# Spreading row scalars with TensorE, and a reordered sparse attention stage, in a two-model transformer stack

## The chip, the cores and the metric

The kernel runs on one core of a Trainium2 chip. The metric is the device time of one execution, in microseconds (us). The weights come from device memory in every execution, about 226 MB of reads.

## The reference

Two small stacks follow one another on a sequence of 512 tokens with 1024 features. The first has a pooling and state space mixer ("even"), a gated convolution mixer ("odd") and a norm ("fn"). The second has two layers, each with a gated feed-forward block ("ffa"), a mixer ("mix"), and a second feed-forward block ("ffb"). The mixer of layer 0 is differential attention beside a recurrent mixer; that of layer 1 is the sparse attention beside an mLSTM. What the change touches is this:

```python
def rmsnorm(x, w, eps=NORM_EPS):
    xf = x.astype(jnp.float32)
    y = xf * lax.rsqrt(jnp.mean(xf * xf, axis=-1, keepdims=True) + eps)
    return (y * w.astype(jnp.float32)).astype(x.dtype)
...
def compress_blocks(z, pe, w1, w2):
    n_cmp = (T - CMP_BLOCK) // CMP_STRIDE + 1
    idx = CMP_STRIDE * np.arange(n_cmp)[:, None] + np.arange(CMP_BLOCK)[None, :]
    blocks = (z[:, :, idx] + pe).reshape(B, G, n_cmp, CMP_BLOCK * d)
    return jax.nn.gelu(blocks @ w1) @ w2
...
    # native_sparse_attention, per block of queries: three softmax branches
    pc = jnp.where(mc, jax.nn.softmax(jnp.where(mc, sc, NEG_INF), axis=-1), 0.0)
    o_cmp = jnp.einsum('bghqn,bgne->bghqe', pc.astype(dt), v_cmp)
    ...
    return gi[..., 0:1] * o_cmp + gi[..., 1:2] * o_slc + gi[..., 2:3] * o_win
```

## The kernel before

Activations lie transposed: features on 128 partitions, the 512 tokens along the free axis, so `x` is eight tiles of 128x512. Every dense product is in split half precision: a weight chunk of 128x1024 is loaded on SP's queue into `st` (L271), ScalarE makes the high half `wh` (L281), VectorE the low half `wl` (L282), and TensorE adds three products per 128-row block, wh·xh, wh·xl, wl·xh (`form1`, L298 to L300, 24 matmuls for one output tile; `form2`, L316 to L318, the same with tokens on the partitions). Three `st` and three pairs `wh`, `wl` are in flight. Each output tile takes one of the eight accumulator banks (`b0` to `b7` in the program, `b` in the rows); the feed-forward blocks use seven of them (`mm=7`), so TensorE can work seven output tiles ahead of the engine that reads them.

Norms are applied late. `norm` scales `x` by its gain into `hh`, `hl`, and the dense products start on that at once. Meanwhile ScalarE squares, VectorE adds (`nsum`, L358), TensorE sums over partitions with a column of ones (L362), and GpSimd takes the power -0.5 (L335). This gives one scalar per token, four columns on 128 partitions (`r`, `rhoc`). To multiply an output tile it has to be a row of 512, repeated on all partitions. `spread` does that: either `rows` (L330) transposes each column, broadcast to 128, on TensorE into a bank and ScalarE copies it out (L378), or, with `far`, SP writes the 2 KB to DRAM (L374) and reads them back broadcast to 128 partitions (L375). The result is `rho`, by which VectorE multiplies each output (L324), and `rb`, which the next norm uses. Before the change all four feed-forward blocks use `far` for both; the two mixers of the second stack use it for `rb` alone. The first feed-forward block also takes in the norm "fn", so it needs two rounds of moments (L362 twice), and scales `x` itself by a spread `rb` in between (L430).

In the last mixer the steps are listed by hand (`START1`, `MIX1`): `s` makes keys with a rotary turn (`rope`: four DMAs `swap` of 64 KB on SP, two products on GpSimd, L988 and L989, a sum on VectorE, L990), `n` values, `f` gates, `c` one compressed branch (0 for keys, 1 for values), `q` a pair of query heads in all three branches, `v`, `k`, `g`, `h` belong to the mLSTM. A compressed branch takes the dense output `sm`, moves it with four DMAs into `zst`, GpSimd adds the position term (`zb`, four adds, L1483), and TensorE multiplies by four chunks of 512 KB, `w` (32-bit matmuls, L1492, 62 columns).

For each pair of heads `nsa_pair` goes through 12 units (four blocks of queries, three branches): scores (L1562), mask and row maximum in one instruction (L996), maximum times -0.125 (L997), exponential (L998), transposes (L1577), a split into halves on ScalarE and VectorE (L1580, L1581), values (L1586). After the third branch of a block of queries six VectorE instructions weigh and add the branches (L1594, L1596).

The order in which each engine issues is set when the program is built: a scheduler places the instructions by a simulated timeline, and some carry a high priority. Each engine then works strictly in its own order, and a waiting instruction holds up all behind it, on SP's queue of DMAs too.

Of the kernel before, what the change touches and what calls it, by code (L numbers as in the profile page):

```python
# [10 lines left out]
F32 = mybir.dt.float32  # L11
F16 = mybir.dt.float16
AF = mybir.ActivationFunctionType
ALU = mybir.AluOpType
# [3 lines left out]
P = 128  # L18
T = 512
# [13 lines left out]
START1 = [('s', 0), ('n', 1), ('c', 0), ('s', 1), ('f', 0), ('c', 1)]  # L33
# [5 lines left out]
PS = 4096.0  # L39
MIX1 = [('q', 0), ('v', 0), ('k', 0), ('g', 0), ('g', 1), ('k', 2), ('h', 0), ('k', 3), ('h', 1), ('g', 3), ('q', 1), ('k', 1), ('q', 2), ('g', 2), ('q', 3), ('v', 1), ('h', 2), ('h', 3)]  # L40
# [144 lines left out]
class Net:  # L185
    def __init__(self, ctx, tc, A, out, taps=None):
        self.tc, self.nc, self.A, self.out = tc, tc.nc, A, out
        self.taps = taps or {}
        nc = self.nc
# [6 lines left out]
        self.rb = self.inv = self.fn = None  # L196
# [136 lines left out]
    def pow(self, x, e, n=4):  # L333
        r = self.small([P, n], "nr2")
        self.nc.gpsimd.tensor_tensor(r, x, (self.half if e < 0 else self.plus)[:, :n], op=ALU.pow)  # L335
        return r
# [44 lines left out]
    def norm(self, i, exact=False, far=False):  # L381
# [4 lines left out]
        g = self.norms[:, i]  # L386
        if exact:
            self.reciprocal()
# [20 lines left out]
        r = self.pow(v, -0.5)  # L409
# [5 lines left out]
        if self.fn is not None:  # L415
# [4 lines left out]
            v = self.small([P, 4], "nv2")  # L420
# [3 lines left out]
            R = self.spread(r, "rb", True)  # L424
            r = self.pow(v, -0.5)
            V.tensor_mul(t, t, r)
        self.rhoc, self.rho = t, self.spread(t, "rho", far)
# [4 lines left out]
        self.reciprocal(v, r)  # L432
        return hh, hl

    def reciprocal(self, v=None, r=None):
        now = v is None
        if now:
            v = self.moments()
            r = self.pow(v, -0.5)
        self.rb = self.spread(r, "rb", not now and self.inv is not None)  # L440
# [38 lines left out]
    def ffn(self, tag, ni, last=0):  # L479
        nc = self.nc  # L480
        with ExitStack() as c:
# [3 lines left out]
            hh, hl = self.norm(ni, far=True)  # L485
# [506 lines left out]
    def soft(self, tk, ps, mask, n, mx, ls, tag, bufs):  # L992
# [476 lines left out]
    def compress(self, s, K, sp, cw, zt):  # L1469
        nc, A = self.nc, self.A  # L1470
        V, G = nc.vector, nc.gpsimd
# [67 lines left out]
    def nsa_pair(self, i, K, nk, yh, yl, q):  # L1539
# [27 lines left out]
        def values(qt, j):  # L1567
# [5 lines left out]
            for hb, pe in enumerate(st.pop((qt, j))):  # L1573
                ps = self.aux()
                at = nk.tile([P, 2, 4, P], F16, name="nat", bufs=3)
                for kt, (k0, kn) in enumerate(ks):
                    nc.tensor.transpose(ps[0:kn, kt * P:(kt + 1) * P], pe[:, k0:k0 + kn], self.ident)  # L1577
                kn, nb = ks[0][1], len(ks)
                v = ps[0:kn, :nb * P].rearrange("p (a b) -> p a b", b=P)
                nc.scalar.activation(at[0:kn, 0, :nb], v, AF.Copy, scale=PS)  # L1580
                V.scalar_tensor_tensor(at[0:kn, 1, :nb], v, PS, at[0:kn, 0, :nb], op0=ALU.mult, op1=ALU.subtract)  # L1581
                for kt in range(nb):
# [228 lines left out]
```

## Time and profile before

| | |
|---|---|
| median of the runs | 2630.56 us (2622.67, 2630.56, 2630.58) |
| profiled execution | 2621.48 us |
| its span, first to last instruction | 2619.7 us |
| mean granted TensorE clock | 0.967 |
| HBM read | 225.57 MB, 89 GB/s over the span |

The profile is of one execution. The busy time of TensorE counts a matmul from its issue to its modelled end, and matmuls overlap; so the distance between starts, and gaps in which nothing runs, tell more than the duration of one. A row of a view in windows gives, for each engine, the busy us and the number of instructions in that stretch, then the granted clock (1.00 is 2.4 GHz, 0.50 is 1.2 GHz).

### The profile page before, as it was taken

Reading aid. Unit: us, or ns where it says so; the run is one execution under the profiler, and the core shown is the slowest. Engines: PE = TensorE matmul, PEld = TensorE weight load, DVE = VectorE, ACT = ScalarE, POOL = GpSimd, SP = SyncE. Lnnn points to the kernel's source line nnn. Section 1 sums busy time; section 2 is a strip of 40 time slices with the busy share of each in tenths; the row PEclk is TensorE's granted clock in tenths of the full one; section 3 lists DMA queues with packets and bytes.
Section 4 is the critical chain, followed back from the end, with each engine's and each line's share of the span. In section 5 each row is a group of like instructions: output and inputs, shape, how many; then the busy total and the mean of one; then the engine's idle time right before and its main releaser. Section 6 shows DMA issues by size and latency. Waiting matters only on the chain.

```text
span 2619.7 us, 36948 instructions
## 1 busy us (share of the span) xinstructions
PE 2489.5 (95%) x14409; PEld 1267.5 (48%) x14409; DVE 1413.3 (54%) x2623; ACT 937.8 (36%) x1619; POOL 722.5 (28%) x625
## 2 busy tenths in 40 slices
PE   6998989989999999999999999999979999999998
PEld 3554434434444556664444444444455555444445
DVE  8945897643333777766333334333335777643334
ACT  3123665423322333334323223332223565433222
POOL 4811861133310333322333103332012110143300
PEclk9889999989999999999999999999989999899999
DMA  4223221233333421123333333333343101333334
GB/s 161 80 55 114 85 68 41 93 96 98 104 110 119 109 70 51 37 63 120 113 99 102 100 103 108 101 105 97 103 119 103 61 24 37 73 117 104 101 99 126
DMA packets 116247, 240.59 MB, mean 92 GB/s; under 512 B 44904, under 2 KB 54248, under 8 KB 116072
## 3 DMA queue, kind: packets, MB, share of 16 engines
q1 hardware_dynamic: 100416, 229.84, 29.1%
q10 hardware_dynamic: 15656, 8.39, 1.2%
q8 instruction: 113, 1.85, 0.3%
q14 instruction: 62, 0.51, 0.1%
HBM read 225.57 MB, written 7.36 MB: 89 GB/s over the span
## 4 chain that ended last, share of the span: by engine, by line
PE 70%; issue 9%; DVE 8%; DMA 5%; POOL 5%; ACT 2%; SPq 1%; POOLq 0%; ACTq 0%; DVEq 0%
PE b L298 14%; PE b L299 14%; PE b L300 14%; PE b L504 4%; PE b L506 4%; PE b L505 4%; POOL cv L921 2%; DVE wl L282 1%; PE b L1149 1%; PE b L1562 1%; PE mm L300 1%; PE mm L299 1%; PE mm L298 1%; PE b L1492 1%; PE b L1065 1%
## 5 line engine op out<-in xcount | busy, mean ns | idle before, releaser
L298 PE MATMUL b<-hh,wh 128*128 128x512 f16 x2096 | 799.6, 383 | 34.7 <-ACT hh L289 7.8
L300 PE MATMUL b<-hh,wl 128*128 128x512 f16 x2096 | 799.6, 382 | 4.1 <-DVE wl L282 4.1
L299 PE MATMUL b<-hl,wh 128*128 128x512 f16 x2096 | 801.8, 383 | 0.4 <-POOL hl L290 0.4
L281 ACT ACTIVATE wh<-st 128x1024 f16<-128x1024 f32 (+6 forms) x432 | 421.9, 978 | 1047.6 <-PE b L299 651.2
L282 DVE SCALAR_TENSOR_TENSOR wl<-st,wh 128x1024 f16<-128x1024 f32 (+6 forms) x432 | 507.5, 1176 | 324.0 <-ACT wh L281 323.2
L299 PEld LDWEIGHTS <-wh 128*128 128x128 f16 x2320 | 229.6, 99 | 303.8 <-issue 47.2
L298 PEld LDWEIGHTS <-wh 128*128 128x128 f16 x2320 | 230.3, 99 | 297.4 <-issue 28.8
L300 PEld LDWEIGHTS <-wl 128*128 128x128 f16 x2320 | 229.9, 99 | 291.6 <-issue 21.6
L504 PE MATMUL b<-fh,wh 128*128 128x512 f16 x660 | 250.1, 379 | 0.0
L505 PE MATMUL b<-fl,wh 128*128 128x512 f16 x660 | 250.1, 379 | 0.0
L506 PE MATMUL b<-fh,wl 128*128 128x512 f16 x660 | 250.1, 379 | 0.0
L493 POOL TENSOR_TENSOR sg<-sg,rho 128x512 f32<-128x512 f32 x88 | 150.8, 1716 | 311.9 <-ACT sg L492 311.9
L290 POOL TENSOR_TENSOR fl<-f,fh 128x512 f16<-128x512 f32 x88 | 142.6, 1620 | 255.2 <-ACT fh L289 255.2
L324 DVE TENSOR_TENSOR sg<-b,rho 128x512 f32<-128x512 f32 x88 | 60.4, 690 | 256.2 <-PE b L300 215.0
L496 DVE SCALAR_TENSOR_TENSOR f<-b,sg 128x512 f32<-128x512 f32 x88 | 60.8, 690 | 237.9 <-PE b L300 225.9
L290 POOL TENSOR_TENSOR hl<-nh,hh 128x512 f16<-128x512 f32 x45 | 57.8, 1291 | 352.2 <-ACT hh L289 352.2
L506 PEld LDWEIGHTS <-wl 128*128 128x128 f16 x660 | 64.6, 98 | 78.0
L505 PEld LDWEIGHTS <-wh 128*128 128x128 f16 x660 | 64.6, 98 | 77.8
L504 PEld LDWEIGHTS <-wh 128*128 128x128 f16 x660 | 64.6, 98 | 77.8
L298 PE MATMUL mm<-hh,wh 128*128 128x512 f16 x224 | 88.1, 397 | 9.3 <-ACT hh L289 7.4
L921 POOL TENSOR_TENSOR cv<-cv,cvt 128x512 f32<-128x512 f32 x60 | 88.3, 1474 | 15.1 <-ACT cvt L920 10.7
L299 PE MATMUL mm<-hl,wh 128*128 128x512 f16 x224 | 88.2, 395 | 3.1 <-DVE hl L290 1.9
(607 smaller groups left out, 3065.9 us busy)
## 6 DMA issues: line engine op xcount, KB each, us to landing
st<-in_gu_a SPq DMA_DIRECT2D x88, 512.0 KB, 3.5
st<-in_gu_b SPq DMA_DIRECT2D x88, 512.0 KB, 3.5
st<-in_dn_b SPq DMA_DIRECT2D x36, 512.0 KB, 3.4
st<-in_dn_a SPq DMA_DIRECT2D x32, 512.0 KB, 3.5
st<-in_od_in SPq DMA_DIRECT2D x24, 512.0 KB, 3.5
st<-in_ab_in SPq DMA_DIRECT2D x22, 512.0 KB, 3.6
st<-in_cd_in SPq DMA_DIRECT2D x16, 512.0 KB, 3.6
st<-in_ev_in SPq DMA_DIRECT2D x15, 512.0 KB, 3.8
```

Source lines behind the costliest of these rows:

```text
L281: nc.scalar.activation(wh[:, s], st[:, s], AF.Copy, scale=WS)
L282: nc.vector.scalar_tensor_tensor(wl[:, s], st[:, s], WS, wh[:, s], op0=ALU.mult, op1=ALU.subtract)
L290: (eng or self.nc.gpsimd).tensor_sub(lo, src, hi)
L298: self.nc.tensor.matmul(ps, wh[:, s], xh[:, k], start=(k == 0), stop=False)
L299: self.nc.tensor.matmul(ps, wh[:, s], xl[:, k], start=False, stop=False)
L300: self.nc.tensor.matmul(ps, wl[:, s], xh[:, k], start=False, stop=(k == kn - 1))
L493: nc.gpsimd.tensor_mul(sg, sg, self.rho)
L496: nc.vector.scalar_tensor_tensor(f, ps, 1.0 / FS, sg, op0=ALU.mult, op1=ALU.mult)
L504: nc.tensor.matmul(ps, wh[:, s], fh[:, k], start=(k == 0), stop=False)
L505: nc.tensor.matmul(ps, wh[:, s], fl[:, k], start=False, stop=False)
L506: nc.tensor.matmul(ps, wl[:, s], fh[:, k], start=False, stop=(k == KF - 1))
L921: G.tensor_add(cv, cv, t)
```

## The change

Four things change.

- `spread` loses its `far` form: every row scalar is spread by four transposes on TensorE and a copy on ScalarE. In the five norms from "ffa" of layer 0 on, the spread of `rb`, which only the next norm needs, is put off until four output tiles later (`later`, `due`, `LATE`).
- A compressed branch is made in two steps, `p` (dense output, DMAs, position term) and `c` (the rest), and other steps stand between them in `START1`. `Q` prepares the first query pair there, and the first `v` moves from `MIX1` to `START1`.
- `soft` folds the factor -0.125 into the masking instruction and takes a minimum, so that L997 goes. It is used in both mixers of the second stack.
- In `nsa_pair` the two heads of a unit share one bank, one copy and one low half where they fit, and the sum over branches is one VectorE product over all three (128x384) and two GpSimd sums. The product's tile shares its buffers with `swap`.

```diff
-START1 = [('s', 0), ('n', 1), ('c', 0), ('s', 1), ('f', 0), ('c', 1)]
+START1 = [('s', 0), ('n', 1), ('p', 0), ('s', 1), ('f', 0), ('Q', 0), ('c', 0), ('p', 1), ('v', 0), ('c', 1)]
+LATE = 4
-MIX1 = [('q', 0), ('v', 0), ('k', 0), ('g', 0), ('g', 1), ...
+MIX1 = [('q', 0), ('k', 0), ('g', 0), ('g', 1), ...
...
+    def later(self):
+        if self.due:
+            self.due[0] -= 1
+            if not self.due[0]:
+                _, v, r = self.due
+                self.due = None
+                self.reciprocal(v, r)
+
     def form1(self, src, kn, xh, xl, w=None):
+        self.later()
...
-    def spread(self, r, name, far=False):
+    def spread(self, r, name):
         t = self.cp.tile([P, T], F32, name=name)
-        if far:
-            d = self.dr.tile([1, T], F32, name=name + "_", bufs=2)
-            self.nc.sync.dma_start(d.rearrange("o (j p) -> (o p) j", j=4), r)
-            self.nc.sync.dma_start(t, d.to_broadcast([P, T]))
-            return t
-        ps = self.rows(r, range(4))
-        self.nc.scalar.activation(t, ps, AF.Copy)
+        self.nc.scalar.activation(t, self.rows(r, range(4)), AF.Copy)
         return t
...
-            R = self.spread(r, "rb", True)
+            R = self.spread(r, "rb")
...
-        self.rhoc, self.rho = t, self.spread(t, "rho", far)
+        self.rhoc, self.rho = t, self.spread(t, "rho")
...
-        self.reciprocal(v, r)
+        if self.inv is None:
+            self.reciprocal(v, r)
+        else:
+            self.due = [LATE, v, r]
...
-        nc.vector.tensor_tensor_reduce(pe[:, :n], ps, mask, 1.0, -3e38, ALU.add, ALU.max, accum_out=mx)
-        nc.vector.tensor_scalar(mx, mx, -0.125, None, op0=ALU.mult)
-        nc.scalar.activation(pe[:, :n], pe[:, :n], AF.Exp, bias=mx, scale=0.125, accum_out=ls)
+        nc.vector.tensor_tensor_reduce(pe[:, :n], ps, mask, -0.125, 3e38, ALU.add, ALU.min, accum_out=mx)
+        nc.scalar.activation(pe[:, :n], pe[:, :n], AF.Exp, bias=mx, scale=-1.0, accum_out=ls)
...
-            for hb, pe in enumerate(st.pop((qt, j))):
+            for hbs in ((0, 1),) if nb < 3 else ((0,), (1,)):
                 ps = self.aux()
                 at = nk.tile([P, 2, 4, P], F16, name="nat", bufs=3)
...
-            for hb in range(2):
-                d = o[:, qt, hb * 64:hb * 64 + 64]
-                V.tensor_scalar(d, po[:, hb, 0], ls[:, hb, 0:1], None, op0=ALU.mult)
-                for j in (1, 2):
-                    V.scalar_tensor_tensor(d, po[:, hb, j], ls[:, hb, j:j + 1], d, op0=ALU.mult, op1=ALU.add)
+            w = nk.tile([P, 2, 3, 64], F32, name="nw", tag="swap")
+            V.tensor_mul(w, po, ls.unsqueeze(3).to_broadcast([P, 2, 3, 64]))
+            d = o[:, qt].rearrange("p (h e) -> p h e", h=2)
+            G.tensor_add(d, w[:, :, 0], w[:, :, 1])
+            G.tensor_add(d, d, w[:, :, 2])
...
-                K["kv"[j] + "cmp"] = self.compress("kv"[j], K, sp, cw, zt)
+                K[j] = self.blocks("kv"[j], cw, zt)
+
+            def compressed(j):
+                K["kv"[j] + "cmp"] = self.compress("kv"[j], K, sp, cw, K[j])
```

The scheduler makes a new order of the whole program from this; up to the first feed-forward block it is the same but for the name of one small tile. In the changed kernel line numbers are higher: L271 is L272, L987 is L994, L1476 is L1482, L1488 is L1499, L1492 is L1503, L330 is L341.

On SP at the start of the first feed-forward block (`in_gu_a`, its first weights; `rb`, `rho` with a number, the copies in DRAM), before:

```order
L271 DMA st<-in_gu_a 128x1024 x8
L374 DMA rb__4326<-nr_4287 128x4x1
L375 DMA rb<-rb__4326 128x512
L271 DMA st<-in_gu_a 128x1024 x3
L374 DMA rb__4345<-nr_4329 128x4x1
L374 DMA rho__4333<-rhoc 128x4x1
L375 DMA rb<-rb__4345 128x512
L375 DMA rho<-rho__4333 128x512
L271 DMA st<-in_gu_a 128x1024 x33
```

and now:

```order
L272 DMA st<-in_od_in 128x1024 x24
L272 DMA st<-in_od_out 128x1024 x8
L272 DMA st<-in_gu_a 128x1024 x44
L272 DMA st<-in_dn_a 128x1024 x2
L272 DMA st<-in_dn_a 128x768
```

Six DMAs are gone, and with them the places where SP stood between weights until a scalar was ready and its copy had landed in DRAM.

On SP in the last mixer, after the weights of the values (`cd_n`) and gates (`cd_g`), before:

```order
L271 DMA st<-in_cd_g 128x320
L271 DMA st<-in_cd_in 128x1024
L374 DMA rb__15544<-nr2n 128x4x1
L375 DMA rb<-rb__15544 128x512
L987 DMA swap<-sm 32x512 x4
L271 DMA st<-in_cd_in 128x1024
L271 DMA st<-in_cd_v 128x1024
L1476 DMA zst<-sm 64x511 x2
L1703 DMA ksx<-ks 64x1024
```

and now:

```order
L272 DMA st<-in_cd_g 128x320
L272 DMA st<-in_cd_in 128x1024
L994 DMA swap<-sm 32x512 x4
L272 DMA st<-in_cd_in 128x1024
L272 DMA st<-in_cd_v 128x1024
L1482 DMA zst<-sm 64x511 x2
L272 DMA st<-in_cd_v 128x1024
L994 DMA swap<-sm 32x512 x2
L1723 DMA ksx<-ks 64x1024
```

The turn of the keys (`swap`) and the move of the compressed branch (`zst`) no longer stand behind the two DMAs of `rb`.

On TensorE at the first matmuls of the compressed keys (`g` are the gates, `w` with a number one 512 KB chunk), before:

```order
L317 MATMUL b_15957<-wl,hh 128x160
L318 LDWEIGHTS hl
L318 MATMUL b_15957<-wh,hl 128x160
L1492 MATMUL b_15754<-zb,w_15755 128x62 x8
L1492 MATMUL b_15754<-zb,w_15765 128x62 x8
L1492 MATMUL b_15754<-zb,w_15775 128x62 x8
L1492 MATMUL b_15754<-zb,w_15785 128x62 x8
L298 LDWEIGHTS wh
```

and now:

```order
L328 MATMUL b_15875<-wl,hh 128x160
L329 LDWEIGHTS hl
L329 MATMUL b_15875<-wh,hl 128x160
L341 MATMUL b_15952<-ident,nrk 128x128 x4
L1503 MATMUL b_16003<-zb,w_16004 128x62 x7
L1448 MATMUL b_15904<-ident,g_15538 4x128
...
L311 MATMUL b_15966<-hh,wl 128x512
L1503 MATMUL b_16003<-zb,w_16004 128x62
L1503 MATMUL b_16003<-zb,w_16014 128x62 x8
L309 LDWEIGHTS wh
```

The 24 dense matmuls of the second keys now stand ahead of this place, where before they came after all four chunks, and dense work stands between the chunks.

## Rows read from the trace of the kernel before

**Rows 1.** the page's first part: busy us, share, instructions.

```profile
PE 2489.5 (95%) x14409; PEld 1267.5 (48%) x14409; DVE 1413.3 (54%) x2623; ACT 937.8 (36%) x1619; POOL 722.5 (28%) x625
```

**Rows 2.** the view in windows, whole core; steady feed-forward is 600:650.

```profile
500.00:552.00 52.00, 40.81 (x175) 18.91 (x174) 25.34 (x38) 16.01 (x21) 7.94 (x7) 0.87 0.28 79
600.00:650.00 50.00, 50.00 (x233) 22.68 (x232) 18.92 (x20) 15.46 (x20) 17.20 (x10) 1.00 0.32 96
850.00:1240.00 390.00, 376.30 (x3516) 230.52 (x3515) 277.27 (x654) 142.94 (x283) 113.42 (x107) 0.98 0.28 75
...
1596.00:1606.00 10.00, 8.27 (x38) 3.46 (x37) 6.10 (x7) 5.85 (x8) 6.63 (x5) 1.00 0.31 108
1929.13:1940.50 11.37, 9.35 (x101) 8.48 (x98) 4.32 (x5) 2.48 (x4) 1.34 (x1) 0.85 0.34 47
1940.50:1953.60 13.10, 0.00 (x1) 0.01 (x1) 3.70 (x3) 2.52 (x3) 7.69 (x7) 0.58 0.43 120
1953.60:1968.40 14.80, 14.16 (x65) 13.85 (x66) 0.32 (x2) 0.00 (x0) 0.62 (x1) 0.50 0.62 195
1968.40:2008.00 39.60, 36.64 (x220) 23.57 (x221) 19.29 (x36) 10.64 (x14) 14.28 (x12) 0.90 0.37 114
2008.00:2250.00 242.00, 227.06 (x1797) 130.18 (x1797) 181.48 (x671) 133.71 (x416) 26.72 (x24) 0.94 0.13 40
2250.00:2310.00 60.00, 54.90 (x249) 24.39 (x248) 37.69 (x49) 27.93 (x39) 21.55 (x15) 0.97 0.47 118
```

**Rows 3.** chain that ended last, pieces in order: start, us, what.

```profile
508.30 7.62 DMA rb__4326<-nr
...
531.47 8.67 DMA rho__4333<-rhoc
540.15 4.78 DMA rho<-rho__4333
...
1927.23 8.38 DMA rb__15544<-nr2n
1935.63 5.09 DMA rb<-rb__15544
1940.79 7.47 DMA zst<-sm
...
1950.78 2.09 POOL ks L290
```

**Rows 4.** timeline of TensorE, 522 to 547: start, us, idle before, releaser.

```profile
527.25 0.99 PE L362 MATMUL b<-ones,nsum 128*128 128x1 f32 x4 [3.84 <-DVE nsum L358]
...
545.70 0.59 PE L298 MATMUL b<-hh,wh 128*128 128x512 f16 x1 [7.35 <-DVE sg L324]
```

**Rows 5.** timeline of VectorE, 505 to 531.

```profile
520.51 2.08 DVE L430 SCALAR_TENSOR_TENSOR x<-x,norms,rb 128x512 f32<-128x512 f32 x3 [7.84 <-DMA rb<-rb__4326]
```

**Rows 6.** line L330 in 1900 to 2000: min, median, max ns.

```profile
L330 PE MATMUL b<-ident,rhoc x4: 272/272/275, 1928.5 to 1928.9; 128*128 128x128 f32 x4
```

**Rows 7.** timeline of SP's queue, 1926 to 1945.

```profile
1936.06 2.42 SPq L987 DMA_DIRECT2D swap<-sm  x4
```

**Rows 8.** timeline of GpSimd, 1930 to 1994.

```profile
1944.00 1.26 POOL L988 TENSOR_TENSOR sm<-sm,c_rope 128x512 f32<-128x512 f32 x1 [10.84 <-DMA swap<-sm]
...
1948.39 2.38 POOL L1483 TENSOR_TENSOR zb<-zst,pe_k 128x248 f32<-128x248 f32 x2 [1.92 <-DMA zst<-sm]
...
1952.83 1.39 POOL L1483 TENSOR_TENSOR zb<-zst,pe_k 128x248 f32<-128x248 f32 x2
```

**Rows 9.** groups by line, TensorE, 2003 to 2009: busy us, mean ns.

```profile
L1492 PE MATMUL b<-zb,w 128*128 128x62 f32 x32 | 3.8, 276 | 1.5 <-POOL nq L290 1.5
```

**Rows 10.** groups by line and shape, VectorE, 2008 to 2250.

```profile
L1596 DVE SCALAR_TENSOR_TENSOR no<-b,nls,no 128x64 f32<-128x64 f32 x64 | 17.4, 272 | 0.5
...
L997 DVE TENSOR_SCALAR nmx<-nmx 128x1 f32<-128x1 f32 x96 | 11.8, 141 | 0.3
...
L1581 DVE SCALAR_TENSOR_TENSOR nat<-b,nat 128x384 f16<-128x384 f32 x16 | 8.7, 549 | 2.0 <-ACT nat L1580 1.9
```

More of the change, by code (lines that the diff above doesn't have):

```diff
@@ L386, in norm @@
         g = self.norms[:, i]
+        assert not self.due
         if exact:
-            self.reciprocal()
+            v = self.moments()
+            self.reciprocal(v, self.pow(v, -0.5))
         if self.fn is not None:
@@ L408, in norm @@
                 v = self.moments()
-        r = self.pow(v, -0.5)
+        keep = lambda: self.cp.tile([P, 4], F32, name="nrk", bufs=3)
+        r = self.pow(v, -0.5, r=keep())
         t = self.cp.tile([P, 4], F32, name="rhoc", bufs=2)
@@ L419, in norm @@
                 w = self.moments(gain, 0.0)
-            v = self.small([P, 4], "nv2")
+            v = self.cp.tile([P, 4], F32, name="nv", bufs=4)
             V.tensor_mul(v, r, r)
@@ L431, in norm, with reciprocal @@
             self.fn = None
-        self.reciprocal(v, r)
+        if self.inv is None:
+            self.reciprocal(v, r)
+        else:
+            self.due = [LATE, v, r]
         return hh, hl
[L435 to L440, printed above, removed]
+    def reciprocal(self, v, r):
+        self.rb = self.spread(r, "rb")
         self.inv = self.cp.tile([P, 4], F32, name="inv", bufs=2)
@@ L1572, in values @@
             ks = [(0, 31)] if j == 0 else [(kt * P, P) for kt in range(qt + 1)]
-            for hb, pe in enumerate(st.pop((qt, j))):
+            kn, nb = ks[0][1], len(ks)
+            pes = st.pop((qt, j))
+            for hbs in ((0, 1),) if nb < 3 else ((0,), (1,)):
                 ps = self.aux()
                 at = nk.tile([P, 2, 4, P], F16, name="nat", bufs=3)
[L1576 to L1582, printed above, removed]
-                    for a, c in ((0, 0), (0, 1), (1, 0)):
-                        v = K["vcmp"][:, c, g * 64:g * 64 + 64] if j == 0 else (
-                            K["nv"][:, c, kt, (j - 1) * P + g * 64:(j - 1) * P + g * 64 + 64])
-                        nc.tensor.matmul(po[:, hb, j], at[0:kn, a, kt], v, start=(kt + a + c == 0),
-                                         stop=(kt == nb - 1 and a == 1))
+                for e, hb in enumerate(hbs):
+                    for kt, (k0, _) in enumerate(ks):
+                        b = e * nb + kt
+                        nc.tensor.transpose(ps[0:kn, b * P:(b + 1) * P], pes[hb][:, k0:k0 + kn], self.ident)
+                na = len(hbs) * nb
+                v = ps[0:kn, :na * P].rearrange("p (a b) -> p a b", b=P)
+                nc.scalar.activation(at[0:kn, 0, :na], v, AF.Copy, scale=PS)
+                V.scalar_tensor_tensor(at[0:kn, 1, :na], v, PS, at[0:kn, 0, :na], op0=ALU.mult, op1=ALU.subtract)
+                for e, hb in enumerate(hbs):
+                    for kt in range(nb):
+                        for a, c in ((0, 0), (0, 1), (1, 0)):
+                            v = K["vcmp"][:, c, g * 64:g * 64 + 64] if j == 0 else (
+                                K["nv"][:, c, kt, (j - 1) * P + g * 64:(j - 1) * P + g * 64 + 64])
+                            nc.tensor.matmul(po[:, hb, j], at[0:kn, a, e * nb + kt], v, start=(kt + a + c == 0),
+                                             stop=(kt == nb - 1 and a == 1))
             if j < 2:
@@ L1773, in mix1 @@
             for step, n in START1 + MIX1:
-                dict(c=packed, s=keys, n=vals, f=gates, Q=query, q=quer, k=qk, v=values, g=gate, h=head)[step](n)
+                dict(p=packed, c=compressed, s=keys, n=vals, f=gates, Q=query, q=quer, k=qk, v=values, g=gate, h=head)[step](n)
             for k in CD_OUT:
```

23 lines of the change are left out of this document (13 added, 10 removed).

## The prediction

> **What bounds the kernel now.** I read the page's engine list first: TensorE is busy 95% of the span, the next engine (VectorE) 54% [rows 1]. Then the windows: in a feed-forward block TensorE runs 233 matmuls in 50 us at full clock, 0.215 us each, with no gap [rows 2], so there nothing but fewer matmuls helps. The change removes no dense matmul. What it can win is time in which TensorE stands, and time at 1.2 GHz after it stood. The windows find these in few places: the start of the first feed-forward block (500 to 552), the start of the sparse attention (1929 to 2008), its inner stretch (2008 to 2250), and little in the starts of the later blocks. The chain of waits names the cause in the first two: the trips of a row scalar through DRAM, and the move of the compressed keys [rows 3]. The timelines give what each engine waited for.
>
> **First feed-forward block.** The trip of `rb` begins at 508.30 and VectorE's scaling of `x` at 520.51, 12.2 us later [rows 3, 5]. In VectorE's order the last two sums of the second round of moments stand behind that scaling, so TensorE, which must sum them over partitions, stands 3.84 us [rows 4]. Then the trip of `rho`, 531.47 to 544.93, is longer than the seven banks last, and TensorE stands 7.35 us more [rows 3, 4]. In all, the 175 matmuls of 500 to 552 would take 37.6 us at the steady rate and took 52: 14.4 us lost, idle and half clock together [rows 2].
> In the new order TensorE does the first moments, 52 dense matmuls (11.2 us), the second moments, 20 more, the transposes of `rb`, 22 more, the transposes of `rho`. So `rho` is asked for about 94 x 0.215 = 20.2 us after the first moments where its arrival came at 544.93 (540.15 + 4.78, rows 3), some 37 us after `rb`'s trip began, and the sums no longer stand behind the scaling. From just ahead of that trip's start (508.30), say 507, this is 527 to 529, before the banks ran out (538.35, less the 3.84 of idle before it: 534.5). Neither idle stays. What is late next is `wl`: the eight scalings now stand between two of them on VectorE, eight times 0.69 us (2.08 for three, rows 5) is 5.5 us against 5.2 us for one output tile, with two pairs ahead; I allow 1 us. Gain 13.4; bounds 8 (if a bank still runs dry) and 14.4.
>
> **Later feed-forward blocks.** There the trip ends within the seven banks; only a `wl` or `wh` queued behind the first use of `rho` is late. 1596 to 1606 has 1.7 us idle, and 2250 to 2310 has 5.1, of which I put 3 on `rho` [rows 2]. Gain 4.7; bounds 0 and 7.
>
> **Price of the spreads.** Eleven spreads leave DRAM: three in the first block, two in each of the three others, one `rb` in each of the two mixers. Four transposes start within 1928.5 to 1928.9 and take 0.272 us each, pipelined [rows 6]: 0.5 us of TensorE for each spread, 5.5 in all, and none of it hidden, since TensorE is the bound. Each also holds all that stands behind it if the power on GpSimd is late; the new order puts 26 dense matmuls (5.6 us) between moments and `rho` in the later blocks, against about 3 us of small work, so I take no wait; up to 1.5 us each, 16 in all, stays in the range.
>
> **Start of the sparse attention.** Loss before, by window [rows 2]: 2.0 idle and about 1 from the clock up to 1940.5; 13.1 idle; then the 64 matmuls of the compressed keys take 14.8 us at 1.2 GHz, where 32 of the same take 3.8 us at full clock [rows 9], so 7.2 lost; then 3.0 idle and 4.0 from a clock of 0.90. Sum 30.3.
> The 13.1 us end with the position term: SP's queue stood 8.38 us for `rb`, then read it back (1935.63), then issued the swaps (1936.06) and, last, `zst` at 1940.79 [rows 3, 7]; GpSimd took the swapped keys at 1944.00 and finished two pairs of adds, with the split of `ks` in between, at 1954.2 [rows 3, 8]. Without `rb` that chain moves up by something between 0 and 8.4 us; I take 5.5, what lies between the swaps' issue and the keys' being ready when the first product with `rho` is out, a little after 1930. So `zb` is ready near 1948. TensorE does the second keys first (24 x 0.215 = 5.2 us, partly in the 2.0 idle) and one spread, and comes to the compressed keys near 1944.2. It stands 4 us instead of 13.1 (bounds 1 and 9.4). A standstill like this costs some 2 us of half clock (500 to 552 lost 0.13 x 52 = 6.8 us of clock with two of them, idle time included). From there the four chunks have dense work between them, so a late chunk or a late gate row hides in part; I leave 4 us for these. Loss after 10, gain 20; bounds 7 (9.4 idle, 7.2 half clock, 7 of waits) and 27.
>
> **Inner stretch of the sparse attention.** 242 us, 15 idle, clock 0.94 [rows 2]. The 96 scalings by -0.125 go: 96 x 0.141 = 13.5 us of VectorE. The 96 instructions of the branch sum (0.272 each, 26 us) become 16 products over 384 columns, near 0.55 us as the split of 384 columns takes [rows 10], 9 us. Thirty-two of 96 copies and low halves merge with a neighbour. VectorE sheds over 30 of 181 us, but TensorE is the bound there too, and its waits on VectorE are a part of the 15 us idle. Against it stand 32 sums on GpSimd, which no row shows at this size: adds of 248 columns took 0.70 to 1.2 us each [rows 8], so 0.35 to 0.6; they run beside other work but for the last ones before the transposes of the output, where they replace VectorE instructions of about the same length. And 40 of the matmuls that filled this stretch now stand before it. I take a gain of 6; bounds -8 and 16.
> GpSimd's adds show a cost of sharing: the same two adds took 2.38 us while VectorE made low halves `wl`, and 1.39 us after [rows 8], 0.5 us more for each add. The Trainium skill (SBUF — State Buffer, "SBUF: two separate sides") says that GpSimd shares a pair of ports with VectorE, and that a VectorE instruction with two SBUF inputs and a GpSimd instruction lock each other out for the whole of an instruction. By that rule the trace's 2.38 us is no accident, since `wl` is made of `st` and `wh`, both in SBUF; the low halves of the softmax read one of their inputs from a bank, and would not lock. This is the third rival below.
>
> **Differential attention** (850 to 1240): the order is new in detail, the mix of work is the same, 13.7 us are idle [rows 2]. I take 0; bounds -6 and 6.
>
> **Sum.** 13.4 + 4.7 + 20 + 6 - 5.5 = 38.6 us from the profiled 2621.5: 2582.9. The median of the timed runs lies 9 us above the profiled one, with one run at 2622.67 beside it; I do not know which the changed kernel's median will meet, and add 2: 2585.
>
> **Rivals.**
> 1. The compressed keys still come late (chance 0.17). For: `zst` now stands behind two weight loads of 512 KB on SP, and GpSimd's order around it is unchanged; 8.38 of standstill is an upper end of what goes. Against: the second keys are ahead in any case. Gain 7 there instead of 20, and spreads that wait 0.5 us each: 2585 + 13 + 6 = 2604.
> 2. More comes back (0.13): the clock stays full through the whole start and the inner stretch gives 16: 2585 - 7 - 10 = 2568.
> 3. The sums on GpSimd and VectorE hold each other up all through the inner stretch (0.05): 32 sums at 0.5 us more each (2.38 against 1.39 for two) is 16 us on the chain that the transposes of the output wait for: 2585 + 16 = 2601. Against: the dense steps in this stretch are few, and so is `wl`. By the skill's rule, named above, the lock would come with `wl` alone, which is why the chance is small.
> 4. Slower than before (0.04): the branch product takes `swap`'s two buffers, so the turn of the next query pair must wait for the sums of the pair before, and nothing covers it. The whole chain from swaps to split took 16.8 us for `ks` (1936.06 to 1950.78 + 2.09, rows 3, 7). Three of them in the open, with the clock at half behind each (7.2 us lost at most, as above), are 3 x 24 = 72 us: 2585 + 72 = 2657. It decides from about 12 us each on. Against: the new order has dense work at those places.
> That the spreads do not pay at all is no rival: the gaps of 3.84 and 7.35 us name them.
>
> **How the numbers follow.** The forecast has 0.61, with its own range 2572 to 2600. The range 2562 to 2611 takes in rivals 2 and 3 and the first, and most of what the unknown order of the mixers can do; the slower case stays outside. Within 0.3% of 2630.6 (about what repeated timings of this kernel differ by) means 2622.7 to 2638.5: 0.05, from rival 1 with a bad order elsewhere. Faster 0.91, slower 0.04.
>
> **What would show it.** Right: no wait of TensorE for `nsum` or `sg` after the first moments at 507; the idle before the first compressed matmul at 1 to 9 us, with dense work between chunks; the granted clock of 1929 to 2008 above 0.85 throughout; the inner stretch 0 to 16 us shorter. Wrong: a wait of TensorE at the transposes of `rhoc` or `nrk` of over 1 us, a gap of over 9 us before the compressed keys, VectorE waiting for GpSimd's `no`, or swaps late on SP with TensorE idle.

## The result and the profile after

The changed kernel takes 2562.23 us (median of 2556.68 to 2567.23) against 2628.84: the ratio is 0.975, with a 95% interval of 0.9722 to 0.9778. Beside other runs on another chip it is 0.977 (0.9746 to 0.9794). Forecast were 2585 with a range of 2562 to 2611: the direction is right, the time lies 0.23 us inside the range's lower edge, and the gain is half as large again as forecast. The profiled execution spans 2558.1 us (2619.7 before).

The page's first part, of the changed kernel, answers to [rows 1]:

```profile
PE 2462.0 (96%) x14453; PEld 1259.9 (49%) x14453; DVE 1397.3 (55%) x2383; ACT 940.7 (37%) x1598; POOL 734.6 (29%) x657
```

To see where the time went, both programs are cut at the first sum over partitions of each norm (L362 before, L373 now). The view in windows, kernel before: first feed-forward block, first mixer, two feed-forward blocks, last mixer, last feed-forward block. The first number after a window is its length, the last three are the granted clock, the DMA share and GB/s.

```profile
506.00:866.50 360.50, 349.31 (x1604) 158.74 (x1604) 138.09 (x164) 105.78 (x132) 85.16 (x60) 0.98 0.35 107
866.50:1237.10 370.60, 356.90 (x3423) 221.25 (x3422) 267.03 (x634) 135.87 (x273) 109.80 (x100) 0.98 0.27 70
1237.10:1580.30 343.20, 342.62 (x1593) 155.68 (x1592) 128.91 (x140) 104.73 (x129) 82.43 (x52) 1.00 0.34 103
1580.30:1924.30 344.00, 342.27 (x1614) 156.28 (x1612) 126.84 (x139) 101.73 (x127) 82.82 (x53) 1.00 0.35 104
1924.30:2277.30 353.00, 317.58 (x2363) 191.81 (x2361) 236.89 (x753) 166.21 (x463) 61.19 (x52) 0.90 0.22 66
2277.30:2598.40 321.10, 317.77 (x1561) 152.50 (x1561) 117.88 (x128) 98.34 (x120) 76.38 (x46) 1.00 0.36 108
```

The same six stages of the changed kernel:

```profile
502.90:848.30 345.40, 345.40 (x1616) 158.41 (x1615) 137.01 (x164) 107.65 (x135) 84.91 (x60) 1.00 0.36 110
848.30:1224.80 376.50, 360.72 (x3425) 226.11 (x3425) 265.62 (x602) 136.00 (x274) 111.00 (x100) 0.98 0.24 69
1224.80:1568.20 343.40, 343.40 (x1601) 156.73 (x1601) 128.96 (x140) 105.84 (x131) 82.70 (x52) 1.00 0.34 102
1568.20:1910.90 342.70, 342.70 (x1621) 157.29 (x1620) 126.72 (x139) 103.11 (x129) 82.58 (x53) 1.00 0.34 103
1910.90:2218.60 307.70, 291.81 (x2368) 178.46 (x2366) 220.69 (x545) 163.74 (x432) 72.55 (x84) 0.98 0.25 75
2218.60:2536.90 318.30, 318.30 (x1569) 153.56 (x1569) 118.47 (x128) 99.16 (x122) 76.43 (x46) 1.00 0.36 108
```

Subtract the lengths: 15.1, -5.9, -0.2, 1.3, 45.3 and 2.8 us, 58.4 together. In all four feed-forward blocks TensorE's busy time now equals the window: it stands nowhere, and the list of its waits in them is empty. The last mixer brings three quarters of the gain. It falls into a start and a rest; the cut is after 520 of its matmuls, the same count in both kernels (not quite the same matmuls, since the new list moves some). Before, then after:

```profile
1924.25:2013.85 89.60, 70.89 (x523) 55.50 (x521) 31.87 (x64) 18.81 (x31) 25.90 (x22) 0.79 0.40 112
2013.85:2277.33 263.48, 246.77 (x1842) 136.37 (x1840) 205.02 (x690) 147.47 (x433) 35.29 (x30) 0.94 0.16 50
```

```profile
1910.94:1976.93 65.99, 62.57 (x523) 47.33 (x521) 34.09 (x58) 19.77 (x31) 21.68 (x22) 0.95 0.53 164
1976.93:2218.64 241.71, 229.23 (x1845) 131.10 (x1846) 186.60 (x487) 143.94 (x402) 50.87 (x62) 0.99 0.17 50
```

The start gains 23.6 us, the rest 21.8. What the first compressed matmuls wait for, answering to the 13.1 us window of [rows 2], stands in TensorE's timeline of the changed kernel, and SP's queue there answers to [rows 7] and the 1940.79 of [rows 3]:

```profile
1931.30 2.00 PE L1503 MATMUL b<-zb,w 128*128 128x62 f32 x14 [2.63 <-POOL zb L1489]
```

```profile
1917.24 3.43 SPq L994 DMA_DIRECT2D swap<-sm  x4
...
1921.88 1.16 SPq L1482 DMA_DIRECT2D zst<-sm  x2
```

Counted from the stage's first sum over partitions, the swaps leave after 6.3 us (11.8 before) and the first compressed matmul runs after 20.4 (29.4 before).

### The profile page after: what moved, and what is told of

It is laid out like the page before. It is cut to its first block, busy times and chain, and to the rows that moved or that the text cites. A ratio compares the mean times of both kernels' runs of the same rounds, so it can differ in the third digit from the quotient of the medians.

```text
span 2558.1 us, 36794 instructions
## 1 busy us (share of the span) xinstructions
PE 2462.0 (96%) x14453; PEld 1259.9 (49%) x14453; DVE 1397.3 (55%) x2383; ACT 940.7 (37%) x1598; POOL 734.6 (29%) x657
## 4 chain that ended last, share of the span: by engine, by line
PE 82%; DVE 7%; issue 4%; POOL 4%; DMA 2%; ACT 1%; SPq 0%; POOLq 0%; ACTq 0%; DVEq 0%
PE b L310 16%; PE b L309 16%; PE b L311 16%; PE b L513 6%; PE b L512 6%; PE b L511 6%; POOL cv L928 3%; PE b L1155 1%; DVE wl L283 1%; PE b L1573 1%; PE mm L311 1%; PE mm L310 1%; PE b L1593 1%; PE mm L309 1%; PE b L1268 1%
## 5 line engine op out<-in xcount | busy, mean ns | idle before, releaser
L309 PE MATMUL b<-hh,wh 128*128 128x512 f16 x2096 | 795.4, 382 | 22.2 <-ACT hh L290 8.2
L283 DVE SCALAR_TENSOR_TENSOR wl<-st,wh 128x1024 f16<-128x1024 f32 (+6 forms) x432 | 512.7, 1188 | 331.1 <-ACT wh L282 330.3
L309 PEld LDWEIGHTS <-wh 128*128 128x128 f16 x2320 | 229.4, 99 | 288.4 <-issue 19.7
L309 PE MATMUL mm<-hh,wh 128*128 128x512 f16 x224 | 87.2, 393 | 10.6 <-ACT hh L290 8.7
```

What stands on the lines that cost most here:

```text
L283: nc.vector.scalar_tensor_tensor(wl[:, s], st[:, s], WS, wh[:, s], op0=ALU.mult, op1=ALU.subtract)
L309: self.nc.tensor.matmul(ps, wh[:, s], xh[:, k], start=(k == 0), stop=False)
```

## The experiments

Every run is compared with the kernel before on its own chip. The medians of that kernel were 2616.21 to 2628.84 us in these series, so a total in us that an expectation names is good to some 10 us only, and the stages say more. All times but the ratios and the totals are from the one profiled execution; "start" and "rest" are the two parts of the last mixer, with the granted clock. Three runs have one and the same order of TensorE in the last mixer (the changed kernel, e8, e12): there the start took 61.9 to 66.0 us (clock 1.00 and 0.95), and the rest 241.7 to 242.5. The cuts of code show a run's edit against the changed kernel.

| run | ratio (95% interval) | first ff block | first mixer | start | rest |
|---|---|---|---|---|---|
| before | 1 | 360.5 | 370.6 | 89.6 (0.79) | 263.5 (0.94) |
| changed | 0.975 (0.9722 to 0.9778) | 345.4 | 376.5 | 66.0 (0.95) | 241.7 (0.99) |
| e1 spread | 0.9966 (0.9952 to 0.998) | 345.4 | 381.2 | 83.3 (0.82) | 266.8 (0.93) |
| e2 split | 1.0014 (1.0 to 1.0029) | 361.3 | 368.2 | 71.9 (0.91) | 273.5 (0.88) |
| e3 both | 0.9918 (0.9883 to 0.9953) | 345.4 | 380.7 | 65.3 (0.95) | 275.5 (0.89) |
| e4 no start | 0.9899 (0.9874 to 0.9924) | 345.5 | 379.3 | 85.2 (0.78) | 249.5 (0.97) |
| e5 old softmax | 0.9843 (0.9817 to 0.9869) | 345.5 | 387.2 | 64.9 (0.95) | 246.3 (0.99) |
| e6 heads apart | 0.9879 (0.9856 to 0.9901) | 345.5 | 373.5 | 65.2 (0.95) | 267.4 (0.90) |
| e7 old sum | 0.9818 (0.9797 to 0.9839) | 345.5 | 373.6 | 65.9 (0.95) | 247.8 (0.99) |
| e8 far rb, mixer 0 | 0.9856 (0.9835 to 0.9877) | 345.4 | 390.8 | 66.0 (0.95) | 242.5 (0.98) |
| e9 shared bank | 0.9893 (0.9866 to 0.9921) | 345.5 | 374.6 | 65.7 (0.95) | 278.4 (0.89) |
| e10 two buffers | 0.9781 (0.9753 to 0.9809) | 345.4 | 376.3 | 65.7 (0.95) | 248.5 (0.98) |
| e11 last sums | 0.9773 (0.975 to 0.9796) | 345.4 | 375.9 | 62.6 (0.97) | 244.4 (0.97) |
| e12 changed again | 0.977 (0.9746 to 0.9794) | 345.5 | 379.3 | 61.9 (1.00) | 241.9 (0.99) |

**The parts by themselves (e1 to e4).** e1 is the kernel before with the new `spread` and `later`:

```diff
-START1 = [('s', 0), ('n', 1), ('p', 0), ('s', 1), ('f', 0), ('Q', 0), ('c', 0), ('p', 1), ('v', 0), ('c', 1)]
+START1 = [('s', 0), ('n', 1), ('p', 0), ('c', 0), ('s', 1), ('f', 0), ('p', 1), ('c', 1)]
...
-            for hbs in ((0, 1),) if nb < 3 else ((0,), (1,)):
+            for hbs in ((0,), (1,)):
... (soft, the branch sum and the place of ('v', 0) as before)
```

Expected: 

> The kernel before with the spreads on TensorE and the late rb alone; the start list, the softmax chain, the pairs and the branch sum are as before. Both theories: the first feed-forward block gains 14 to 15 us, the later blocks 2 to 4. Theory (the start of the sparse attention gains by its new list, SP's freedom from rb moves the compressed keys up by some 5 us only): standstill before the compressed keys 6 to 9 us instead of 13.1, their matmuls still mostly at 1.2 GHz, in all 2590 to 2600. Rival (rb on SP was the whole cause): standstill under 3 us, half clock in 1910 to 1995 under 10 us, in all 2570 to 2582.

Measured: the first block to the tenth as in the changed kernel; 7.21 us of standstill before the compressed keys, inside the theory's 6 to 9:

```profile
1940.11 5.17 PE L1504 MATMUL b<-zb,w 128*128 128x62 f32 x23 [7.21 <-POOL zb L1490]
```

The total misses both ranges: the first mixer lost 10.6 us, and the start still has a clock of 0.82. e2 keeps the DMAs and changes the list alone:

```diff
-    def spread(self, r, name):
+    def spread(self, r, name, far=False):
...
+        if far:
+            d = self.dr.tile([1, T], F32, name=name + "_", bufs=2)
...
-            hh, hl = self.norm(ni)
+            hh, hl = self.norm(ni, far=True)
... (soft, the heads and the branch sum as before; START1 and MIX1 as changed)
```

Expected: 

> The kernel before with the two-step compressed branch and the new start list alone; rb and rho of the feed-forward blocks go through DRAM as before, and rb of the mixers too. Theory: first feed-forward block as before (14 us lost), the start of the sparse attention gains 12 to 20 of the 25 us that the changed kernel gains there, in all 2600 to 2612. Rival (the wait for rb on SP holds the keys whatever stands beside them): the gain there is under 6 us, in all 2615 or more.

Measured: the start gained 17.7 us, as the theory had it, with 9.45 us of standstill before the compressed keys:

```profile
1964.16 4.10 PE L1507 MATMUL b<-zb,w 128*128 128x62 f32 x18 [9.45 <-POOL zb L1493]
```

And yet the kernel is not faster, since the rest of the mixer grew by 10.0 us at a clock of 0.88 (before 0.94) and the second stage stood longer in that execution (189.2 us against 175.1). e3 joins the two:

```diff
-            for hbs in ((0, 1),) if nb < 3 else ((0,), (1,)):
+            for hbs in ((0,), (1,)):
...
-            w = nk.tile([P, 2, 3, 64], F32, name="nw", tag="swap")
...
+            for hb in range(2):
+                d = o[:, qt, hb * 64:hb * 64 + 64]
+                V.tensor_scalar(d, po[:, hb, 0], ls[:, hb, 0:1], None, op0=ALU.mult)
... (soft as before)
```

Expected: 

> The changed kernel with the softmax chain, the separate heads and the six-instruction branch sum of before, so spreads and start list alone. Theory (the three edits of the inner stretch are worth what the two traces show there, some 15 to 20 us, idle and half clock together): 15 to 20 us slower than the changed kernel, 2573 to 2580, with two or more stretches of half clock over 6 us after 2000. Rival (the inner stretch got better because the start left it in another order and fed it more dense work): within 5 us of the changed kernel, 2557 to 2567.

```profile
1937.35 3.25 PE L1504 MATMUL b<-zb,w 128*128 128x62 f32 x14 [3.21 <-POOL zb L1490]
```

In the start the two add up: 6.3 for the spreads and 17.7 for the list are 24.0, together 24.3 (each from one execution, and a start is known to some 4 us). The half clock that the theory foresaw is there, in three stretches of 17 to 21 us after 2000, but the total is above the 2580 of the theory and far from the rival: the inner edits are worth 33.8 us of the rest here (275.5 to 241.7), not 15 to 20. e4 is the changed kernel with the old list:

```diff
-START1 = [('s', 0), ('n', 1), ('p', 0), ('s', 1), ('f', 0), ('Q', 0), ('c', 0), ('p', 1), ('v', 0), ('c', 1)]
+START1 = [('s', 0), ('n', 1), ('p', 0), ('c', 0), ('s', 1), ('f', 0), ('p', 1), ('c', 1)]
```

Expected: 

> The changed kernel with the start list of before (both steps of a compressed branch together, first query and first value in their old places); spreads and inner edits stay. Theory: the start loses 14 to 20 us against the changed kernel, 2572 to 2582, standing 6 to 9 us before the compressed keys. Rival (the spreads alone free the start): within 5 us of the changed kernel.

Its start lost 19.2 us, with 6.11 of standstill before the compressed keys; the rest lost 7.8 more, so the total (2592.79) is 11 us above the range. The rival falls. What follows from e1 to e4: the start was understood, the rest was not. The list alone makes the rest 10 us longer; beside the inner edits it makes it 8 us shorter (249.5 in e4, 241.7).

**Which inner edit (e5 to e7).** Each takes one edit out of the changed kernel.

```diff
-        nc.vector.tensor_tensor_reduce(pe[:, :n], ps, mask, -0.125, 3e38, ALU.add, ALU.min, accum_out=mx)
+        nc.vector.tensor_tensor_reduce(pe[:, :n], ps, mask, 1.0, -3e38, ALU.add, ALU.max, accum_out=mx)
+        nc.vector.tensor_scalar(mx, mx, -0.125, None, op0=ALU.mult)
...
```

Expected: 

> The changed kernel with the softmax chain of before (maximum, then a product by -0.125 in an instruction of its own, in both mixers). The three inner edits together are worth 34 us in the inner stretch beside the new start list (270 us without them, 237 with). Theory A (the chain from scores to transposes is what TensorE waits for, and L997 is one of its links): this alone gives back 15 to 25 of the 34, in all 2575 to 2585. Theory B (VectorE's total time in the stretch decides, wherever it is shed): 13.5 of some 33 us of VectorE come back, so 10 to 14 us, 2570 to 2574. Theory C (it is another edit): under 5 us, below 2565.

Measured in the rest: 4.6 us longer, theory C. The total (2575.16) stands where theory A had it, but for another reason: in the profiled execution 10.7 us came in the first mixer, where the same function is used, and 9.8 in the two stages before the first feed-forward block, whose orders did not change.

```diff
-            for hbs in ((0, 1),) if nb < 3 else ((0,), (1,)):
+            for hbs in ((0,), (1,)):
```

Expected: 

> The changed kernel with the two heads of a unit apart again (own bank, own copy, own low half for each; 32 more of both). Theory A (the length of the chain of one unit): the merged copy makes a unit wait for one copy and one low half instead of two, 5 to 12 us come back, 2565 to 2572. Theory B (VectorE's total): 32 low halves of 0.3 us or so, 6 to 10 us. Theory C (a bank less for each small unit lets scores run ahead, and this is the main part): 15 us or more, 2575 and up.

25.7 us longer in the rest: the size of theory C, whose mechanism e9 tests.

```diff
-            V.tensor_mul(w, po, ls.unsqueeze(3).to_broadcast([P, 2, 3, 64]))
-            d = o[:, qt].rearrange("p (h e) -> p h e", h=2)
-            G.tensor_add(d, w[:, :, 0], w[:, :, 1])
...
+                for j in (1, 2):
+                    V.scalar_tensor_tensor(d, po[:, hb, j], ls[:, hb, j:j + 1], d, op0=ALU.mult, op1=ALU.add)
```

Expected: 

> The changed kernel with the branch sum as six VectorE instructions again. Theory A: the sums matter only where the output's transposes wait for them, once for each pair (1.85 us waits of no before, 0.9 and 1.8 now): within 4 us of the changed kernel, 2556 to 2564. Theory B (VectorE's total: 26 us instead of 9): 12 to 17 us come back, 2570 to 2577. Rival: GpSimd's sums are the slower way, and the six instructions give 2 to 5 us more: 2552 to 2556.

6.1 us longer in the rest, between the ranges of A and B; the rival falls. The total (2570.43) lies in B's range, but 6.8 us of it came in the first stage, whose order did not change. So VectorE's total (theory B) does not decide. By its busy time in the rest (186.6 us in the changed kernel) e7 puts back 11.8 us and costs 6.1, e5 puts back 6.2 and costs 4.6, e6 puts back 3.6 and costs 25.7.

**Why the pairs matter (e6, e9, e10).** ScalarE's copies and VectorE's low halves in the rest, groups by line, heads apart (e6):

```profile
L1596 ACT ACTIVATE nat<-b 31x128 f16<-31x128 f32 (+4 forms) x96 | 34.1, 373 | 45.1 <-PE b L1593 42.7 <-PE b L1603 1.6
...
L1597 DVE SCALAR_TENSOR_TENSOR nat<-b,nat 31x128 f16<-31x128 f32 (+4 forms) x96 | 38.0, 415 | 10.8 <-ACT nat L1596 10.1
```

and in the changed kernel:

```profile
L1596 ACT ACTIVATE nat<-b 128x512 f16<-128x512 f32 (+3 forms) x64 | 29.9, 480 | 25.8 <-PE b L1593 25.0 <-PE b L1603 0.3
...
L1597 DVE SCALAR_TENSOR_TENSOR nat<-b,nat 128x512 f16<-128x512 f32 (+3 forms) x64 | 34.0, 547 | 6.4 <-ACT nat L1596 6.2
```

Four microseconds each on two engines that are not the bound. The windows over the second, third and fourth pair of heads (from the first scores on `kcmp` to the transposes of the output) show what they turn into. First e6, then the changed kernel:

```profile
2073.00:2111.80 38.80, 36.61 (x382) 27.23 (x382) 29.64 (x112) 27.70 (x104) 7.98 (x13) 0.94 0.06 15
2117.80:2175.30 57.50, 56.70 (x422) 30.66 (x422) 37.94 (x123) 29.58 (x98) 7.87 (x12) 0.88 0.18 56
2179.20:2217.60 38.40, 34.89 (x268) 20.46 (x269) 20.82 (x84) 20.78 (x72) 4.79 (x9) 0.60 0.00 1
```

```profile
2063.00:2099.10 36.10, 34.11 (x372) 23.79 (x371) 28.60 (x101) 27.02 (x90) 7.32 (x12) 1.00 0.06 16
2107.40:2144.50 37.10, 34.99 (x355) 21.75 (x355) 31.28 (x106) 28.42 (x97) 7.51 (x11) 1.00 0.19 51
2152.70:2188.50 35.80, 32.25 (x323) 18.73 (x323) 25.06 (x87) 20.91 (x69) 3.62 (x8) 1.00 0.08 23
```

The same windows for L309 alone (one in three of the dense matmuls of `form1`), e6 and the changed kernel:

```profile
2073.00:2111.80 38.80, 0.38 (x1) 0.23 (x2) 0.94 0.06 15
2117.80:2175.30 57.50, 15.48 (x40) 3.99 (x41) 0.88 0.18 56
2179.20:2217.60 38.40, 0.00 (x0) 0.15 (x1) 0.60 0.00 1
```

```profile
2063.00:2099.10 36.10, 0.76 (x2) 0.20 (x2) 1.00 0.06 16
2107.40:2144.50 37.10, 5.17 (x14) 1.47 (x15) 1.00 0.19 51
2152.70:2188.50 35.80, 6.86 (x18) 1.90 (x19) 1.00 0.08 23
```

With the heads apart the scheduler puts 40 of these beside the third pair and none beside the fourth; merged, 14 and 18. (Beside the second pair stand some 50 dense matmuls of `form2` in either.) The fourth pair without dense work ran at a clock of 0.60: TensorE is busy 34.89 of 38.40 us and still takes longer than the changed kernel does for the pair and 18 x 3 dense matmuls. What it did before the clock fell, and while it was low (e6):

```profile
2173.30:2180.10 6.80, 3.89 (x20) 1.52 (x18) 3.22 (x4) 1.55 (x3) 4.30 (x5) 1.00 0.16 49
2180.10:2210.80 30.70, 29.93 (x188) 16.48 (x189) 16.56 (x76) 18.29 (x67) 2.08 (x5) 0.50 0.00 1
```

Just before the fall it stood 2.9 of 6.8 us, in waits of 0.2 to 1.3 us; then it ran at 1.2 GHz for 30.7 us in which it hardly stood at all. The Trainium skill (TensorE: Matmul & The Clock Gate, "A second HAM failure mode: psum-queue depth-cycling") tells of a kernel whose clock swings because TensorE stands briefly and often between groups of matmuls. The short waits before the fall agree; that the clock then stays low through 30.7 us of nearly unbroken work is not explained by them.

TensorE's idle time over the whole last mixer differs by little (19.2 us in e6, 15.9 in the changed kernel), the granted clock by 0.09 of 267 us, 24 us of the 25.7.

e9 shares the bank, but leaves each head its own copy and low half:

```diff
-            for hbs in ((0, 1),) if nb < 3 else ((0,), (1,)):
-                ps = self.aux()
+            for hb in range(2):
+                if hb == 0 or nb > 2:
+                    ps = self.aux()
+                o0 = hb * nb if nb < 3 else 0
...
```

Expected: 

> The changed kernel with the two heads of a small unit in one bank, but with a copy and a low half for each (so the 32 more instructions of both engines that the run with heads apart had, without its 32 more banks). With heads apart the last mixer took 332.6 us, 59 of them at half clock, against 307.7 and 13. Theory (banks: with two for a unit the scores of the next unit wait until transposes are read): the mixer takes 307 to 316, in all 2557 to 2568. Rival (the number of instructions on the chain from transposes to values): 325 to 335, in all 2575 to 2588.

36.7 us longer in the rest, more than with the heads apart, and 344.1 for the mixer: above both ranges. Its second, third and fourth pair, L309 alone:

```profile
2069.90:2119.50 49.60, 0.38 (x1) 0.28 (x2) 0.83 0.05 12
2126.00:2185.90 59.90, 16.25 (x42) 4.41 (x43) 0.91 0.19 56
2189.40:2228.40 39.00, 0.00 (x0) 0.15 (x1) 0.64 0.00 1
```

Sharing the bank alone brings nothing back. The dense work went the same way as in e6, and the clock too. e9 also puts the second head's transposes behind the first head's values in program order, so it does not single out the merged copy, nor does it rule out that banks have a part.

```diff
-                at = nk.tile([P, 2, 4, P], F16, name="nat", bufs=3)
+                at = nk.tile([P, 2, 4, P], F16, name="nat", bufs=2)
```

Expected: 

> The changed kernel with two buffers instead of three for the halves of the softmax weights. A merged unit fills one buffer for two heads, so three buffers hold up to six heads where the kernel before held three. Theory (banks or instructions matter, not these buffers): the last mixer within 5 us of 307.7. Rival (the merged form gained because it can be further ahead in these buffers): 10 us or more are lost, 318 and up.

6.8 us longer in the rest, and 314.2 for the mixer: between the two. The buffers have a part, a small one.

**The first mixer (e8).**

```diff
-        if self.inv is None:
-            self.reciprocal(v, r)
+        if self.inv is None or far:
+            self.reciprocal(v, r, far)
...
-            hh, hl = self.norm(4)
+            hh, hl = self.norm(4, far=True)
```

Expected: 

> The changed kernel with rb of the first mixer alone through DRAM, written at once, as before; all else as changed. The first mixer took 370.5 us before, 368.2 with the start list alone, 376.5 in the changed kernel and 379 to 381 in three kernels with the spreads. Theory (the spread of rb on TensorE is the cause: its transposes take a bank and a place in every engine's order): the mixer is back at 366 to 370, the second feed-forward block unchanged, in all 2549 to 2553 by the profile, faster than the changed kernel. Rival (the order came out worse for another reason, as the short softmax chain): the mixer stays at 375 to 381, in all 2557 or more.

It got 14 us slower at a clock of 0.94, above both ranges of the mixer; the theory falls:

```profile
856.80:1247.50 390.70, 371.12 (x3421) 230.53 (x3420) 267.97 (x602) 135.58 (x273) 106.71 (x100) 0.94 0.25 67
```

With the old softmax the spread on TensorE costs this mixer 10 us (370.6 to 381.2), with the short one it saves 14 (390.8 to 376.5). So neither way of spreading is better in itself; that the new order of the whole is what counts is argued, not shown. (The 390.8 is one execution.) And on one and the same order of TensorE the mixer took 373.5 to 379.3 us (e4, e6, e7, e9 to e12 and the changed kernel), or 380.7 to 387.2 (e1, e3, e5), through the clock.

**A candidate, and the changed kernel again (e11, e12).** TensorE's waits in the rest of the changed kernel name GpSimd's sums (us in total, times, longest):

```profile
PE b L1623 <- POOL no L1613: 2.7, 2, 1.8
```

```diff
-            G.tensor_add(d, w[:, :, 0], w[:, :, 1])
-            G.tensor_add(d, d, w[:, :, 2])
+            S = V if qt == 3 else G
+            S.tensor_add(d, w[:, :, 0], w[:, :, 1])
+            S.tensor_add(d, d, w[:, :, 2])
```

Expected: 

> The changed kernel with the two sums over branches of the last block of queries on VectorE instead of GpSimd (8 of 32 sums). TensorE waits for them there: 2.7 us in two waits in the trace of the changed kernel, 1.8 the longest. Theory: two VectorE sums of 128 columns end sooner, the last mixer gains 1 to 3 us, and the whole is 0.1% below the changed kernel run beside it. Rival (it is VectorE's queue that is long there): no difference, or up to 3 us more.

```profile
PE b L1624 <- DVE no L1614: 3.1, 3, 1.4
```

The longest wait is shorter, their sum is not, the rest is 2.5 us longer than in e12, and the ratio is the changed kernel's own. The theory falls, the rival holds, and no version here beats the changed kernel.

Expected: 

> The changed kernel once more, beside the others on one chip. 0.974 to 0.978 of the kernel before; by the trace the last mixer 305 to 311 us, the first mixer 372 to 378 and the first stage 247 to 255, where equal orders have differed by 3 and 7 us through the clock alone.

Measured as expected but for the last mixer (303.8 us) and the first (379.3), 1.2 and 1.3 us off their ranges.

## Why the prediction was right, and what was mis-sized

- **The range held by 0.23 us, in part by luck.** Two of the four timed runs (2556.68 and 2559.88) lie below its 2562, and the forecast's own 2572 was missed by 10 us. The inner stretch alone was 15.8 us off; the first mixer, slower by 5.9, hid some of that.
- **First feed-forward block: right, a little low.** Forecast 13.4 less three spreads, 11.9; measured 15.1. `rho`'s transposes came at 525.2, which is 528.3 on the old clock (the block starts 3.1 us earlier now); forecast 527 to 529. No `wl` was late. e1 and e3 give 345.4 as well, so the spreads with `later` did it.
- **Later feed-forward blocks: right.** 4.7 less six spreads, 1.7; measured -0.2, 1.3 and 2.8, so 3.9.
- **Price of a spread: too high.** In the block at 1237 0.6 us of idle time went and 0.2 was lost, 0.8 for two spreads; in the one at 1580 1.7 went and 1.3 were won, 0.4 for two: 0.2 to 0.4 each, where I put 0.5. No spread made TensorE wait in these blocks.
- **Start of the sparse attention: right in mechanism, 20 forecast, 23.6 measured.** The spreads alone made the compressed keys 7.5 us earlier (21.8 us after the first sums in e1, 29.4 before); I took 5.5 between 0 and 8.4. The standstill is 2.63 us (4 forecast). The list is worth 17.7 of the 24.3. In e2 TensorE still stood 9.45 us before the compressed keys, but its idle time in the start fell from 18.7 to 9.5 us and its clock rose from 0.79 to 0.91. Rival 1, compressed keys still late, falls.
- **Inner stretch: mis-sized, and the largest miss.** The term was 6, with 16 as its upper bound; measured 21.8 (over the rest, which runs 27 us further than the 2250 of the prediction). I reckoned the shed instructions by their time on VectorE and their part in 15 us of TensorE's idle time. The idle time fell by only 4.2 us (16.7 to 12.5). What I read and did not price is the clock: 0.94 of 263 us leaves some 15.8 us to win on top, and 13 of them came back. VectorE's busy time fell by 18.4 us (205.0 to 186.6), not by over 30, since its short instructions overlap: the 96 scalings of [rows 10] have 11.8 us of busy time, where I took 96 times their mean, 13.5. I also ranked the parts wrongly: the -0.125 product brings 4.6, the sum 6.1, and the merged heads, which I had in one sentence, 25.7.
- **First mixer: 0 forecast, -5.9 measured,** on the bound of its range. On the changed order it took 373.5 to 379.3 over the runs, which is 3 to 9 us more than in the one execution before. What causes it is not settled: e8 speaks against the spread as such.
- **Rival 2 (2568) is what came nearest;** it named the clock of the start and 16 in the inner stretch, and I gave it 0.13. Rival 3: the GpSimd sums took 0.46 and 0.51 us, inside the 0.35 to 0.6 that I worked out without such an effect, VectorE never waited for `no`, and the product took 0.55 as forecast. (I named `wl` as the only instruction of VectorE here that reads two tiles outside the banks; `nsum` and `nh` are others.) The sums:

```profile
L1613 POOL TENSOR_TENSOR no<-no,nw 128x128 f32<-128x128 f32 x16 | 8.1, 508 | 1.2
L1612 POOL TENSOR_TENSOR no<-nw 128x128 f32<-128x128 f32 x16 | 7.4, 460 | 93.9 <-DVE nw L1610 87.3 <-DVE nls L1608 6.6
```

  Rival 4, the product's buffers, shows nowhere: no idle time of TensorE in the rest is above 1.8 us.
- **First stage.** The remaining 3 us between the two profiled executions lie in the first stage (251.0 and 247.9), whose order did not change; over the runs it took 247.9 to 255.0. They are not the change's.

Open: whether the merged heads keep the clock up by themselves, or because dense work then stands elsewhere. For the dense work speaks that with separate copies (the kernel before, e1 to e3, e6, e9) the rest has nine stretches of 17 to 31 us at half clock, and eight of them hold no dense matmul. Heads apart do not lower the clock everywhere: in the second pair, from its last dense matmul on, both forms ran alike, e6 first:

```profile
2086.40:2112.50 26.10, 23.41 (x267) 16.66 (x266) 21.58 (x73) 20.83 (x70) 6.62 (x11) 1.00 0.06 17
```

```profile
2075.20:2100.50 25.30, 22.98 (x253) 16.05 (x252) 20.84 (x63) 19.24 (x60) 7.57 (x12) 0.99 0.07 17
```

(The 0.94 of that pair in e6 is half clock that began at 2070.8, ahead of its first scores.) Nor does dense work beside a pair keep the clock up throughout: the kernel before has 28 of L298 beside its last pair, all in the first of these two windows:

```profile
2191.30:2213.60 22.30, 21.85 (x146) 10.39 (x145) 14.78 (x55) 8.43 (x29) 1.16 (x1) 1.00 0.16 54
2213.60:2247.80 34.20, 28.00 (x233) 16.69 (x232) 22.27 (x100) 16.91 (x54) 0.00 (x0) 0.73 0.02 5
```

With merged heads no run goes longer than some 28 us there without dense work, so the two stay unseparated.

## What to carry to other kernels

Where a stretch shows a granted clock well below 1, its price is up to the length times what is missing (24 of the 25.7 us in e6), and an edit off the bound can win that back, so an estimate from idle time alone can be too low. Look at which stretches have no dense matmuls beside them; that a shorter list of small instructions pays by letting a scheduler put dense work there fits the runs, but is not shown. Time an edit by its stage and together with the others: here the start list alone gained the last mixer 7.7 us (353.1 to 345.4 in e2), and beside the spreads and the inner edits 27.0 (334.7 in e4 to 307.7).

## What the runs showed of the hardware

TensorE ran at 1.2 GHz for 30.7 us in which it was busy 29.93 us (e6, 2180.1 to 2210.8), after 6.8 us at full clock in which it was busy 3.89 and its longest wait was 1.3 us. And on one order the clock moved a stage by 6 to 7 us from execution to execution (first mixer 380.7 to 387.2, first stage 247.9 to 255.0), while the dense feed-forward blocks repeated to 0.1 us.
